# Delta rule in a four-layer network: later places for the transfers of the inverse's blocks, two buffers for the inverse, four for its input

## The chip, the cores and the metric

One core of one Trainium2 chip runs the whole program once. The metric is the time of that execution in microseconds (us), as the median of several runs. A profiled execution is shown beside it; all rows below are from that one execution.

## The reference

The network has four layers on 272 tokens (16 learned ones and 256 given), then a second network of two blocks. Layers 0 and 3 mix tokens with a gated delta rule, and only these two call what is changed. For each of 8 heads, in chunks of 64 tokens:

```python
a_strict = where(strict, (k*beta) @ k.T * decay, 0)     # lower triangle
m = a_strict + eye
u = triangular_solve(m, v * beta)
w = triangular_solve(m, k * beta * exp(gc))
# then over the chunks, with a state S (128 x 128) of each head:
v_new = u - w @ S
o = (q * exp(g)) @ S + (q @ k.T * decay) @ v_new
S = S * exp(g_last) + (k * exp(g_last - g)).T @ v_new
```

q, k, v come from one projection of the normalised input, a causal convolution over four tokens, SiLU and a norm; o is normalised, gated by z and projected back to the residual h.

## The kernel before

A stage of the program is one layer: `dn0`, `mlp0`, `da1`, `mlp1`, `lru2`, `mlp2`, `dn3`, then the second network (`blk2`). In a delta stage (`_dn`) the input projection is cut into 16 weight chunks of 1 MB, in the order of `DN_ORDER`: k0 k1 v0 q0 k2 v1 q1 k3 z0 v2 q2 v3 q3 z1 z2 z3. The number is a pair of heads; there are four pairs. A chunk is loaded by SP's queue into `wraw` (three buffers), split by ScalarE and VectorE into a high and a low part (`whi`, `wlo`, three buffers each, line 418 and 421), and used in 48 matmuls into `pm` (line 392). So each stage has 16 x 48 of them, and then 4 x 48 of the output projection (`proj_out`, chunks `dno`): 960.

For each pair the chunk of 128 tokens is the unit of the solve (and the 16 learned tokens are a small one). `dn_keys` forms the strict triangle U (matmuls `ga`, VectorE writes `U`); `dn_blocks` inverts its 16 x 16 diagonal blocks; `dn_merge` joins them to the inverse `Y` by matmuls `gp` and `pp` (six steps in turn, each needs VectorE's or ScalarE's result of the one before); `dn_chain` runs the recurrence (`pvm`, `sp`, then `ksp`, `pv`, `spn`, `po` for either chunk), and `dn_tail` norms, transposes (`oT`) and gates the output for `proj_out`.

`dn_blocks` goes through DRAM to bring blocks to partitions: SP stores U to `ud` (line 940) and loads `X` from it (942); GpSimd (POOL) does 15 steps of elimination on X into `yb` (947 to 954); SP stores `yb` to `yd` (957) and loads `yc` (959), from which `dn_merge` starts. `X` and `yb` have one buffer each.

These are Python generators, one task each. `mm3` calls `tick()` after every eighth matmul, and a tick lets every task run to its next `yield`; `yield n` sleeps n ticks. `finish(task)` ticks, with no matmul between, until a task is done. This makes the order in which the program is written. It is not the order in which the engines get it: the framework that builds the program fills each engine's queue itself, taking what it reckons to be ready, and the earliest written first. On the chip each queue is then worked in that fixed order.

Waits in the written order: `dn_keys` of pair p waits, before U, until the inverse of pair p-2 is merged (there are two `fx` sets, pair p uses set p % 2; one Y for all), and `dn_merge` of pair p waits until pair p-1 has used Y (`solved`).

Of the kernel before, what the change touches and what calls it, by code (L numbers as in the profile page):

```python
# [9 lines left out]
F32 = mybir.dt.float32  # L10
# [290 lines left out]
class Prog:  # L301
# [56 lines left out]
    def act(self, out, a, func, **k):  # L358
        i = self.S.activation(out=out, in_=a, func=func, **k).ins  # L359
        if func in (AF.Exp, AF.Ln):  # L360
            if self.table is not None:
                self.order(i, self.table)
        elif func in (AF.Silu, AF.Sqrt):
            self.other = i
        return i
# [168 lines left out]
    def _dn(self, s, layer, last, e):  # L534
        nc, A, d1 = self.nc, self.A, self.d1
        t0 = NM if last else 0
        w0 = self.chunk(A[f"dnA{s}"][0])
        self.dnc = d1.tile([P, _DNC.n], F32, name="dnc")
        nc.sync.dma_start(out=self.dnc, in_=A["dnc"])
        u, R = self.normed(self.h, f"nmix{layer}", T)  # L540
        y = [d1.tile([P, 4, T], F32R, name=n)[:, :, t0:T] for n in ("yh", "yl")]
        ys = [[a[:, 2 * i:2 * i + 2, :] for a in y] for i in range(2)]
        self.d2 = d2 = e(self.tc.tile_pool(name="d2", bufs=2))
        gates, ready = self.dn_gates(s, u, R)
        self.dn_fixed()
        conv = f"dnconv{s}"
        zs = d1.tile([P, 8, T], F32, name="zs")
        chains, outs, self.ms = [], [], {}
        self.solved = 0
        self.inv, keys, f = [None] * 4, [[] for _ in range(4)], {}  # L550

        def project(nm, p, w):
            ci = "kvq".index(nm)
            f[nm, p] = cv = d2.tile([P, 2, T], F32, tag=nm + "T", name=nm + "T", bufs=4 if nm == "k" else 2)
            for m in range(2):
                ps = self.pm.tile([P, 512], F32, tag="pm", name="pm")[:, 0:T]
                self.mm3(ps, w, 8, 256, m, u)
                raw = d2.tile([P, 3 + T], F32, tag="raw", name="raw")
                self.V.memset(raw[:, 0:3], 0.0)
                self.tt(raw[:, 3:], ps, R, ALU.mult)  # L560
                j = (8, 16, 0)[ci] + 2 * p + m
                self.act(cv[:, m, :], raw[:, 3:3 + T], AF.Copy, scale=self.pc(conv, 72 + j))
                for t in range(3):
                    self.stt(cv[:, m, :], raw[:, t:t + T], self.pc(conv, 24 * t + j), cv[:, m, :], ALU.mult, ALU.add)
            self.act(cv, cv, AF.Silu)
            if nm == "k":
                self.spawn(self.dn_keys(p, cv, gates, ready, keys[p]))

        tails = []
        def load(o):  # L570
            nm, p = o[0], int(o[1])
            return self.chunk(A[f"dnA{s}"][12 + p if nm == "z" else 3 * p + "kvq".index(nm)])

        order = DN_ORDER.split()
        ws = [w0]
        for i, o in enumerate(order):
            nm, p = o[0], int(o[1])
            if i + 1 < len(order):
                ws.append(load(order[i + 1]))
            w = ws[i]  # L580
            if nm != "z":
                project(nm, p, w)
                if nm == "q":
                    on = (d1.tile([P, 2, 2, P], F32, name=f"on{p}"), None if last else d1.tile([48, P], F32, name=f"om{p}"))
                    outs.append(on)
                    chains.append(self.spawn(self.dn_chain(p, f["k", p], f["v", p], f["q", p], gates, keys[p], on, last)))
                continue
            for m in range(2):
                ps = self.pm.tile([P, 512], F32, tag="pm", name="pm")[:, 0:T - t0]
                self.mm3(ps, w, 8, 256, m, (u[0][:, :, t0:T], u[1][:, :, t0:T]))  # L590
                z = d2.tile([P, 3 + T], F32, tag="raw", name="z")[:, t0:T]
                self.tt(z, ps, R[:, t0:T], ALU.mult)
                self.act(zs[:, 2 * p + m, t0:T], z, AF.Silu)
            if p > 1:
                ys.append([d2.tile([P, 2, T], F32R, tag="kT", name=n, bufs=4)[:, :, t0:T] for n in ("yh", "yl")])
            tails.append(self.spawn(self.dn_tail(s, p, chains[p], outs[p], zs, ys[p], t0)))
        ys = [[[a[:, j, :] for b in ys[g:g + 2] for a in (b[i],) for j in range(2)] for i in range(2)] for g in (0, 2)]
        self.proj_out(f"dno{s}", ys, T - t0, [[t] for t in tails], self.add_h(t0))
# [24 lines left out]
    def dn_fixed(self):  # L623

        d1, V = self.d1, self.V
        self.fx = []
        for i in range(2):
            t = dict(U=d1.tile([P, 5, P], F32, name=f"U{i}"), At=d1.tile([48, 48], F32, name=f"Atm{i}"),
                     vm=d1.tile([48, P], F32, name=f"vm{i}"), km=d1.tile([48, 2, P], F32, name=f"km{i}"),
                     Y=d1.tile([P, 4, P], F32, name="Y") if i == 0 else self.fx[0]["Y"])  # L630
            V.memset(t["U"][:, 4, :], 0.0)
            for n in ("At", "vm", "km"):
                V.memset(t[n], 0.0)
            self.fx.append(t)

    def dn_gates(self, s, u, R):
# [115 lines left out]
    def dn_ssq(self, x, out):  # L752

        sp = self.pst("ssq2")
        self.V.memset(sp[:, 4:5], 0.0)
        sq = self.d2.tile([P, 2, T], F32, tag="sq2", name="sq2", bufs=1)
        self.act(sq, x, AF.Square)
        for h, c in self.M4:
            i = 2 * h + c
            self.colsum(sp[:, i:i + 1], sq[:, h, self.CK[1 + c]])  # L760
        for h in range(2):
            self.mm(sp[self.RH[h], 4:5], sq[:, h, 0:16], self.ones[:, 0:1])
        self.V.tensor_scalar_add(out=out, in0=sp[:, 0:5], scalar1=EPS)

    def dn_keys(self, p, kT, gates, ready, keys):

        d2, mm, tt, stt, act, V = self.d2, self.mm, self.tt, self.stt, self.act, self.V
        RH, ck = self.RH, self.CK
        while not ready.done:
            yield  # L770
        rows, bet, gc, ng = gates
        fx = self.fx[p % 2]
        mneg = self.dc("mneg")
        E = d2.tile([P, 2, T], F32, tag="E", name="E")
        Dx = d2.tile([P, 4, P], F32, tag="Dx", name="Dx")
# [20 lines left out]
        V.reciprocal(out=sv, in_=kk)  # L796
        tt(sv, sv, bet[:, p, :], ALU.mult)
        yield
        while p > 1 and self.inv[p - 2] is None:
            yield  # L800
        U = fx["U"]
        ga = self.pst("ga").rearrange("p (a b) -> p a b", a=4)
        gm = self.pst("gm")
# [7 lines left out]
        for r in RH:  # L811
            stt(U[r, 4, r], gm[r, 0:16], sv[r, 4:5], Dm[r], ALU.mult, ALU.mult)
        box = []
        yield from self.dn_blocks(U, box)
        while p and self.solved < p:
            yield
        self.inv[p] = yield from self.dn_merge(U, box[0], fx["Y"])

    def dn_chain(self, p, kT, vT, qT, gates, keys, outs, last):
# [1 line left out]
        M4, RH, ck = self.M4, self.RH, self.CK  # L821
        rows, bet, gc, ng = gates
        on, om = outs
        fx = self.fx[p % 2]
        while len(keys) < 5 or self.solved < p - 1:
            yield
        E, Dx, Dm, sk, sv = keys
# [41 lines left out]
        for h in range(2):  # L869
            r = RH[h]  # L870
            act(ke[:, h, :], kp[:, h, :], AF.Copy, scale=Dx[:, 2 * h, P - 1:P])
            act(km[r, h, :], kp[r, 2, :], AF.Copy, scale=Dm[r, 15:16])
            act(vm[r], kp[r, 3, :], AF.Copy, scale=sk[r, 4:5])
        while self.inv[p] is None:
            yield
        Y, Ym = self.inv[p]
# [55 lines left out]
        stt(ms, ms, 1.0 / P, qf, ALU.mult, ALU.add)  # L932
        self.ms[p] = ms

    def dn_blocks(self, U, box):

        d2, dd, V, G = self.d2, self.dd, self.V, self.G
        q = self.nc.sync
        ud = dd.tile([5, 129, P], F32, tag="ud", name="ud")
        q.dma_start(out=ud[:, 0:P, :].rearrange("m p c -> p m c"), in_=U)  # L940
        X = d2.tile([40, 16, 16], F32, tag="X", name="X", bufs=1)
        q.dma_start(out=X, in_=bass.AP(ud.tensor, ud.offset, [[2064, 40], [P, 16], [1, 16]]))
        yb = d2.tile([40, 16, 2, 16], F32, tag="yb", name="yb", bufs=1)
        yield 6
        t = d2.tile([40, 15, 16], F32, tag="t16", name="t16", bufs=1)
        Y = yb[:, :, 0, :]
        G.memset(Y, 0.0)
        G.memset(yb.rearrange("p a t b -> p (a t b)")[:, 0:512:33], 1.0)
        for k in range(15, 0, -1):
            n = 16 - k  # L950
            o = t[:, 0:k, 0:n]
            G.tensor_tensor(out=o, in0=X[:, 0:k, k:k + 1].broadcast_to([40, k, n]), in1=Y[:, k:k + 1, k:16].broadcast_to([40, k, n]), op=ALU.mult)  # L952
            G.tensor_tensor(out=Y[:, 0:k, k:16], in0=Y[:, 0:k, k:16], in1=o, op=ALU.subtract)  # L953
        G.tensor_copy(out=yb[:, :, 1, :], in_=Y.rearrange("p a b -> p b a"))
        yield 10
        yd = dd.tile([40, 16, 2, 16], F32, tag="yd", name="yd")
        q.dma_start(out=yd, in_=yb)
        yc = d2.tile([P, 5, 2, 16], F32, tag="yc", name="yc")
        q.dma_start(out=yc.rearrange("p m t c -> p m (t c)"), in_=bass.AP(yd.tensor, yd.offset, [[32, P], [4096, 5], [1, 32]]))
        box.append(yc)  # L960
        yield 8

    def dn_merge(self, U, yc, Y):

# [947 lines left out]
```

## Time and profile before

| | us |
|---|---|
| median of 3 runs | 2575.45 (2573.39 to 2577.97) |
| profiled execution: its own time | 2578.68 |
| profiled execution: span of the rows | 2576.5 |
| TensorE (PE) busy in the span | 2520.1 (98%) |
| stage dn0, first gate matmul to end of pair 3's `oT` | 7.1 to 210.3 |
| stage dn3, the same | 1034.6 to 1226.9 |

Rows give times in us from the start of the span, and durations in us unless ns is written. PE is TensorE's matmuls, PEld its weight loads, DVE VectorE, ACT ScalarE, POOL GpSimd, SP the engine whose queue issues the transfers; a q behind an engine means its queue. A row such as `72.21 0.65 PE L392 MATMUL gp<-yw,U ... x32 [3.48 <-...]` is 32 matmuls of line 392 that write `gp` from `yw` and `U`, began at 72.21, took 0.65, after 3.48 in which the engine stood idle; what released it is named behind the arrow, by the profile's inference.

### The profile page before, as it was taken

How to read it: one execution, taken by the hardware profiler on the slowest of the kernel's cores; microseconds unless marked ns; L12 is line 12 of the kernel's file. 1: busy time of each engine (PE TensorE's matmuls, PEld its weight loads, DVE VectorE, ACT ScalarE, POOL GpSimd, SP SyncE). 2: the span in 40 equal slices, each digit the busy share in tenths (PEclk: the TensorE clock that was granted, in tenths of full speed). 3: DMA queues.
4: the chain of work that ended last, by engine and by line, in shares of the span. 5: the costliest groups of instructions: out<-in, count | busy, mean ns of one | idle time of the engine just before them, and what ended most of it. 6: DMA issues, size and time to landing. Idle time of an engine off the chain costs nothing.

```text
span 2576.5 us, 54055 instructions
## 1 busy us (share of the span) xinstructions
PE 2520.1 (98%) x21942; PEld 2449.5 (95%) x21942; DVE 2044.8 (79%) x4613; ACT 1469.6 (57%) x2544; POOL 119.8 (5%) x280
## 2 busy tenths in 40 slices
PE   8899999999999999989999999999999999999998
PEld 8789999999999999979999999999878999999998
DVE  8678967779779976857996887886767978987765
ACT  8776445664457644868654544644655445545544
POOL 1420001000000000331000000000000000000000
PEclk9899999999999999989999999999999999999999
DMA  4326755347545764323875665564314865974553
GB/s 173 114 95 233 281 180 178 132 180 262 196 147 182 262 229 168 116 99 128 291 295 181 234 245 176 197 213 168 128 60 163 325 246 195 327 257 148 180 187 108
DMA packets 89577, 494.56 MB, mean 192 GB/s; under 512 B 18448, under 2 KB 28336, under 8 KB 33264
## 3 DMA queue, kind: packets, MB, share of 16 engines
q1 hardware_dynamic: 89328, 491.10, 54.2%
q8 instruction: 173, 2.83, 0.4%
q14 instruction: 76, 0.62, 0.1%
HBM read 485.10 MB, written 5.96 MB: 191 GB/s over the span
## 4 chain that ended last, share of the span: by engine, by line
PE 88%; DVE 3%; POOL 3%; ACT 2%; DMA 2%; issue 1%; SPq 0%; DVEq 0%; ACTq 0%; POOLq 0%
PE pm L392 81%; POOL t L952 1%; POOL yb L953 1%; PE o L392 1%; DVE wlo L421 1%; ACT L359 1%; DMA wraw<-dnA 1%; PE sp L392 1%; PE ssq L392 0%; PE ga L392 0%; DMA crow<-crow 0%; PE po L392 0%; PE oT L402 0%; DMA X<-ud 0%; ACT whi L418 0%
## 5 line engine op out<-in xcount | busy, mean ns | idle before, releaser
L418 ACT CAST whi<-wraw 128x1024 fp32r<-128x1024 f32 (+1 forms) x767 | 768.8, 1033 | 556.3 <-PE pm L392 319.1
L392 PE MATMUL pm<-ul,whi 128*128 128x258 f32 (+2 forms) x3768 | 1084.2, 288 | 1.5 <-DVE ul L409 0.8
L392 PE MATMUL pm<-uh,whi 128*128 128x258 f32 (+2 forms) x3768 | 1080.2, 287 | 2.9 <-ACT uh L359 2.3
L392 PE MATMUL pm<-uh,wlo 128*128 128x258 f32 (+2 forms) x3768 | 1081.2, 288 | 0.2 <-DVE wlo L421 0.2
L421 DVE TENSOR_TENSOR wlo<-wraw,whi 128x512 fp32r<-128x512 f32 x1511 | 984.2, 690 | 95.5 <-ACT whi L418 92.4
L392 PEld LDWEIGHTS pm<-uh,whi 128*128 128x128 f32 x3768 | 714.5, 190 | 8.3 <-ACT uh L359 2.7
L392 PEld LDWEIGHTS pm<-ul,whi 128*128 128x128 f32 x3768 | 714.3, 190 | 7.5 <-issue 2.8
L392 PEld LDWEIGHTS pm<-uh,wlo 128*128 128x128 f32 x3768 | 714.7, 190 | 6.6 <-issue 4.3
L392 PE MATMUL pm<-hh,wlo 128*128 128x256 f32 (+1 forms) x1904 | 541.5, 284 | 0.0
L392 PE MATMUL pm<-hh,whi 128*128 128x256 f32 (+1 forms) x1904 | 541.4, 284 | 0.0
L392 PE MATMUL pm<-hl,whi 128*128 128x256 f32 (+1 forms) x1904 | 540.4, 284 | 0.0
L392 PEld LDWEIGHTS pm<-hl,whi 128*128 128x128 f32 x1904 | 361.0, 190 | 0.0
L392 PEld LDWEIGHTS pm<-hh,wlo 128*128 128x128 f32 x1904 | 359.0, 189 | 0.0
L392 PEld LDWEIGHTS pm<-hh,whi 128*128 128x128 f32 x1904 | 358.2, 188 | 0.0
L1395 DVE SCALAR_TENSOR_TENSOR wmod<-wmod,crow 128x1024 f32<-128x1024 f32 x144 | 174.1, 1214 | 0.1
L356 DVE TENSOR_TENSOR h<-h,pm 128x272 f32<-128x272 f32 (+1 forms) x192 | 81.8, 428 | 83.4 <-PE pm L392 82.8
L408 ACT CAST hh<-t 128x256 fp32r<-128x256 f32 x110 | 44.5, 405 | 146.0 <-DVE t L353 145.7
L359 ACT ACT_TABLE_LOAD x88 | 112.9, 1283 | 10.0 <-DMA crow<-crow 7.4
L359 ACT ACTIVATE s<-r 128x272 f32<-128x272 f32 (+1 forms) x128 | 53.7, 425 | 71.5 <-DVE r L353 70.3
L359 ACT ACTIVATE t<-t,b 128x256 f32<-128x256 f32 x110 | 55.5, 507 | 64.8 <-DVE t L356 64.7
L356 DVE TENSOR_TENSOR t<-pm,rstd 128x256 f32<-128x256 f32 x220 | 90.6, 413 | 0.0
L353 DVE SCALAR_TENSOR_TENSOR h<-pm,gate,h 128x256 f32<-128x256 f32 x96 | 46.1, 480 | 49.8 <-PE pm L392 49.7
(453 smaller groups left out, 2699.8 us busy)
## 6 DMA issues: line engine op xcount, KB each, us to landing
wraw<-mlp SPq DMA_DIRECT2D x128, 1024.0 KB, 4.9
wmod<-wmod SPq DMA_DIRECT2D x72, 1024.0 KB, 6.3
wraw<-f1i SPq DMA_DIRECT2D x66, 1024.0 KB, 4.8
wraw<-f2i SPq DMA_DIRECT2D x44, 1024.0 KB, 4.9
wraw<-dnA SPq DMA_DIRECT2D x32, 1024.0 KB, 4.9
wraw<-f1o SPq DMA_DIRECT2D x24, 1024.0 KB, 4.8
wraw<-f2o SPq DMA_DIRECT2D x16, 1024.0 KB, 4.8
wraw<-daA SPq DMA_DIRECT2D x12, 1024.0 KB, 4.9
```

The source lines that it names most:

```text
L353: self.V.scalar_tensor_tensor(out=out, in0=a, scalar=s, in1=b, op0=op0, op1=op1)
L356: self.V.tensor_tensor(out=out, in0=a, in1=b, op=op)
L359: i = self.S.activation(out=out, in_=a, func=func, **k).ins
L392: self.PE.matmul(out=out, lhsT=lhsT, rhs=rhs, start=start, stop=stop)
L408: self.S.copy(out=hi, in_=x)
L418: self.S.copy(out=hi[:, k], in_=raw[:, k])
L421: self.V.tensor_sub(out=lo[:, k], in0=raw[:, k], in1=hi[:, k].bitcast(F32))
L952: G.tensor_tensor(out=o, in0=X[:, 0:k, k:k + 1].broadcast_to([40, k, n]), in1=Y[:, k:k + 1, k:16].broadcast_to([40, k, n]), op=ALU.mult)
L953: G.tensor_tensor(out=Y[:, 0:k, k:16], in0=Y[:, 0:k, k:16], in1=o, op=ALU.subtract)
L1395: i = self.V.scalar_tensor_tensor(out=junk, in0=w[:, k, :], scalar=1.0, in1=c[:, r, :], op0=ALU.mult, op1=ALU.mult, accum_out=m[:, j:j + 1])
```

## The change

`dn_blocks` gets the pair's number and sleeps differently. Before: store ud, load X, 6 ticks, POOL, 10 ticks, store yd, load yc, 8 ticks. After: store ud, 4 ticks, wait until the pair before has left POOL's part (`blocked`), load X, 3 ticks, POOL, 16 ticks, store yd, 3 ticks, load yc, 4 ticks. There are four U (one for each pair) and two Y. `dn_keys` no longer waits for the inverse of pair p-2, but for the reads of `dn_chain` of pair p-2 (`read`). `dn_merge` of pair p waits for the merge of pair p-1 and for pair p-2's use of Y. `sq2` shares its buffer with `yf`, which gives back part of the space.

```diff
-        self.solved = 0
+        self.solved = self.read = self.blocked = 0
...
-        for i in range(2):
-            t = dict(U=d1.tile([P, 5, P], F32, name=f"U{i}"), At=d1.tile([48, 48], F32, name=f"Atm{i}"),
-                     vm=d1.tile([48, P], F32, name=f"vm{i}"), km=d1.tile([48, 2, P], F32, name=f"km{i}"),
-                     Y=d1.tile([P, 4, P], F32, name="Y") if i == 0 else self.fx[0]["Y"])
+        for i in range(4):
+            t = dict(self.fx[i - 2]) if i > 1 else dict(
+                At=d1.tile([48, 48], F32, name=f"Atm{i}"), vm=d1.tile([48, P], F32, name=f"vm{i}"),
+                km=d1.tile([48, 2, P], F32, name=f"km{i}"), Y=d1.tile([P, 4, P], F32, name=f"Y{i}"))
+            for n in ("At", "vm", "km") if i < 2 else ():
+                V.memset(t[n], 0.0)
+            t["U"] = d1.tile([P, 5, P], F32, name=f"U{i}")
             V.memset(t["U"][:, 4, :], 0.0)
-            for n in ("At", "vm", "km"):
-                V.memset(t[n], 0.0)
...
-        sq = self.d2.tile([P, 2, T], F32, tag="sq2", name="sq2", bufs=1)
+        sq = self.d2.tile([P, 2, T], F32, tag="yf", name="sq2", bufs=1)
...
-        while not ready.done:
+        while not ready.done or self.read < p - 1:
             yield
...
-        fx = self.fx[p % 2]
+        fx = self.fx[p]
...
-        while p > 1 and self.inv[p - 2] is None:
-            yield
         U = fx["U"]
...
-        yield from self.dn_blocks(U, box)
-        while p and self.solved < p:
+        yield from self.dn_blocks(p, U, box)
+        while p and (self.solved < p - 1 or self.inv[p - 1] is None):
             yield
...
+        self.read = p + 1
         while self.inv[p] is None:
             yield
...
         q.dma_start(out=ud[:, 0:P, :].rearrange("m p c -> p m c"), in_=U)
+        yield 4
+        while self.blocked < p:
+            yield
         X = d2.tile([40, 16, 16], F32, tag="X", name="X", bufs=1)
         q.dma_start(out=X, in_=bass.AP(ud.tensor, ud.offset, [[2064, 40], [P, 16], [1, 16]]))
...
-        yield 6
+        yield 3
...
-        yield 10
+        yield 16
+        self.blocked = p + 1
         yd = dd.tile([40, 16, 2, 16], F32, tag="yd", name="yd")
         q.dma_start(out=yd, in_=yb)
+        yield 3
...
-        yield 8
+        yield 4
```

## Rows read from the trace of the kernel before

**Rows 1.** The page, part 1: busy time, share of the span, instructions.

```profile
PE 2520.1 (98%) x21942; PEld 2449.5 (95%) x21942; DVE 2044.8 (79%) x4613; ACT 1469.6 (57%) x2544; POOL 119.8 (5%) x280
```

**Rows 2.** Windows: length, busy PE, PEld, DVE, ACT, POOL; clock, DMA share, GB/s.

```profile
60.00:100.00 40.00, 32.17 (x436) 28.18 (x435) 25.77 (x77) 26.19 (x51) 16.75 (x47) 0.83 0.38 124
...
160.00:212.00 52.00, 52.00 (x563) 48.13 (x562) 35.01 (x84) 38.04 (x95) 0.00 (x0) 1.00 0.34 111
...
1090.00:1130.00 40.00, 27.97 (x371) 25.20 (x370) 20.34 (x58) 19.91 (x37) 16.48 (x33) 0.74 0.27 93
```

**Rows 3.** Timeline of PE: the long waits inside the two stages.

```profile
72.21 0.65 PE L392 MATMUL gp<-yw,U 32*32 32x32 f32 x32 [3.48 <-DVE raw L559]
...
89.96 1.11 PE L392 MATMUL gp<-yt,U 64*64 64x64 f32 x8 [4.35 <-ACT yt L359]
...
125.12 0.66 PE L392 MATMUL pp<-Y,gs 64*64 64x64 f32 x5 [1.64 <-ACT gs L1027]
...
1115.11 1.11 PE L392 MATMUL gp<-yt,U 64*64 64x64 f32 x8 [11.83 <-ACT yt L359]
```

**Rows 4.** Timeline of ACT before the second and the fourth of these.

```profile
88.28 1.04 ACT L418 CAST whi<-wraw 128x1024 fp32r<-128x1024 f32 x1 [4.72 <-DMA wraw<-dnA]
...
1113.43 1.04 ACT L418 CAST whi<-wraw 128x1024 fp32r<-128x1024 f32 x1 [12.38 <-DMA wraw<-dnA]
```

**Rows 5.** Timeline of SP's queue: transfers in the order of issue.

```profile
44.71 0.34 SPq L415 DMA_DIRECT2D wraw<-dnA  x1
45.15 0.35 SPq L942 DMA_DIRECT2D X<-ud  x1
...
81.55 0.29 SPq L957 DMA_DIRECT2D yd<-yb  x1
81.95 0.34 SPq L415 DMA_DIRECT2D wraw<-dnA  x1
...
1108.23 1.41 SPq L415 DMA_DIRECT2D wraw<-dnA  x3
```

**Rows 6.** Waits of SP's queue, 0 to 240 and 1030 to 1240: total, times, longest.

```profile
SPq L957 <- POOL yb L954: 37.4, 4, 13.9
...
SPq L957 <- POOL yb L954: 50.1, 4, 20.6
```

**Rows 7.** Windows of POOL's run of pair 1, in dn0 and in dn3.

```profile
67.30:81.60 14.30, 10.82 (x186) 10.11 (x185) 9.26 (x31) 9.78 (x16) 11.71 (x33) 0.76 0.20 72
...
1086.30:1106.00 19.70, 16.77 (x276) 15.25 (x274) 17.98 (x51) 14.23 (x23) 17.29 (x31) 0.97 0.13 50
```

**Rows 8.** Windows of the tile pm alone in dn0: PE, PEld, DVE, ACT.

```profile
12.50:72.20 59.70, 45.79 (x331) 42.57 (x331) 4.94 (x12) 0.00 (x0) 0.99 0.42 139
72.30:171.90 99.60, 55.80 (x325) 46.64 (x325) 6.54 (x16) 0.00 (x0) 0.91 0.34 110
172.00:198.20 26.20, 16.66 (x106) 14.05 (x107) 1.74 (x4) 0.00 (x0) 1.00 0.24 81
```

**Rows 9.** The chain that ended last, end of dn0: start, us, what.

```profile
198.28 10.92 PE pm L392 x87
209.20 1.06 PE oT L402 x6
```

**Rows 10.** Windows of the stretches at half clock: one, and the four's sum.

```profile
125.30:132.10 6.80, 6.80 (x37) 5.73 (x37) 3.63 (x11) 4.41 (x10) 0.00 (x0) 0.50 0.26 81
...
sum 40.80, PE 27.03 PEld 24.16 DVE 11.11 ACT 20.06 POOL 6.96; mean PE 6.76 PEld 6.04 DVE 2.78 ACT 5.01 POOL 1.74
```

**Rows 11.** Groups of ACT and DVE, 171.9 to 212: count, busy us, mean ns.

```profile
L359 ACT ACTIVATE on<-on,ms 128x128 f32<-128x128 f32 x12 | 3.9, 392 | 0.5 <-DVE ms L606 0.4
L359 ACT ACT_TABLE_LOAD x3 | 3.8, 1283 | 0.1
...
L353 DVE SCALAR_TENSOR_TENSOR yf<-oT,par,zs 128x272 f32<-128x272 f32 x6 | 3.0, 500 | 3.5 <-PE oT L402 3.3
...
L409 DVE TENSOR_TENSOR yl<-yf,yh 128x544 fp32r<-128x544 f32 x3 | 2.2, 721 | 0.3 <-ACT yh L408 0.3
```

More of the change, by code (lines that the diff above doesn't have):

```diff
@@ L823, in dn_chain @@
         on, om = outs
-        fx = self.fx[p % 2]
+        fx = self.fx[p]
         while len(keys) < 5 or self.solved < p - 1:
@@ L933, in dn_chain, with dn_blocks @@
         self.ms[p] = ms
-    def dn_blocks(self, U, box):
+    def dn_blocks(self, p, U, box):
         d2, dd, V, G = self.d2, self.dd, self.V, self.G
```

## The prediction

> **What bounds the kernel now.** I read the page's busy times first. PE is busy 98% of the span and POOL 5% [rows 1], so a change to POOL's transfers can only give back time in which PE stands still or runs slowly. Windows of the two delta stages show where that is: in the 40 us from 60 and in the 40 us from 1090 PE misses 7.8 and 12.0 us and the clock is granted at 0.83 and 0.74; late in the stage, from 160 to 212, PE misses nothing [rows 2]. PE's timeline gives the waits: 3.48, 4.35 and 1.64 us in dn0 and 11.83 us in dn3, 21.3 us together, all in front of a step of `dn_merge` [rows 3].
>
> The arrow behind the 4.35 and the 11.83 points at ScalarE's `yt`. Going one step back, ScalarE itself had stood 4.72 and 12.38 us at the cast of a weight chunk that had not arrived [rows 4]; it works in order, so `yt` stood behind that cast. Another step back, SP asked for that chunk at 81.95 and 1108.23, directly after the store of yd of pair 1 (and, in dn3, the load of yc) [rows 5]. And SP's waits say why so late: the store of yd stood 13.9 us and 20.6 us for POOL, 37.4 and 50.1 us over the four pairs of a stage [rows 6]. POOL's run of pair 1 takes 14 us in dn0 and 20 us in dn3 [rows 7]. So the chain is POOL, yd at the head of SP's queue, weight load, cast, merge, PE. The 1.64 and the 3.48 us are in front of merge steps too, and I take them for yc that comes late.
>
> Behind each wait the granted clock was at half: four stretches, 40.8 us, PE busy in 27.0 [rows 10], at 0.50, the lower of the two levels (1.2 GHz). At the upper one that work needs 13.5 us less. All that could be given back is then 21.3 + 13.5 = 34.8 us, 1.4% of the span, and any other cost must be set against this.
>
> **The change part by part.** It adds no matmul and no transfer; it moves them in the written order. That is not the order of the queues: the load of a weight chunk that is written four chunks behind X was issued before X [rows 5]. So a later place does not by itself delay a transfer on SP, which is mostly free when the builder picks; the place decides among things that are ready together. On PE, where `pm` matmuls are nearly always ready, it decides a lot.
>
> I counted ticks from the yields (8 `pm` matmuls to a tick, 960 in a stage). Before, the first `gp` of pairs 0 to 3 is written at matmul 296, 408, 544 and 656; after, at 344, 496, 648 and 860. The counted rows agree for the last pair: 331 + 325 = 656 stand before its `gp`, and 331 before pair 0's, which came 35 later than written [rows 8]. Later pairs come out later because the pairs now go through POOL's part one at a time, 3 + 16 = 19 ticks each.
>
> (1) *The early stalls.* Pair 0's `gp` moves from 331 to at least 344, 13 matmuls of 126 ns (10.92/87 [rows 9]), 1.6 us; U of pair 2 with its matmuls comes before it, some 1.2 us (8 matmuls like `oT`'s six in 1.06). Of the 3.48 + 4.35 that leaves some 5; in dn3 18 matmuls and the same U take 3.5 from 11.83. The 1.64, with its stretch of half clock (6.8 busy, so 3.4 [rows 10]), goes: POOL's run of pair 2 no longer waits for a merge, since U has a buffer of its own, and is done long before merge 2. Of the other half clock (10.1) I take 3. Sum: 2.8 + 3.5 + 1.6 + 3.4 + 3 = 14.3; I take 15. The bounds are 0 (SP's order as before) and 34.8 (every stall gone).
>
> Whether more goes hangs on one thing: yd of pair 1 and the next weight load stand side by side in SP's queue [rows 5]. If the later place of yd lets the load pass, both long waits vanish; if the builder reckons POOL's run shorter than the 14 to 20 us [rows 7], yd stays in front. Nothing in the trace of before tells which.
>
> (2) *The end of the stage.* Pair 3's merge is now written at matmul 860, the rest of it behind 888, and from there `finish(tail 3)` ticks 16 times with no matmul between. The last 72 of `proj_out` need that pair. Before, all this stood among 106 `pm` matmuls and PE missed nothing [rows 2, 8]. That PE takes the earlier written first is seen at `oT` of pair 3: 87 matmuls of 10.92 us stand between the last `po` and it [rows 9], in the place that the ticks give (848). So the cover is gone.
> Price of one stage: the 26.2 us from pair 3's `gp` to its last `po` hold 106 x 0.126 = 13.3 of `pm`; of the 12.9 left 2.1 are two other pairs' `oT` and 1.4 eight `kp` by the same price, so 9.4 is PE's part of merge and chain. Bounds of merge and chain without cover: 9.4, as if nothing stood between steps, and 26.2, as now. I take 15.4: 12 steps in turn with 0.5 between (one DVE operation of 500 ns, or an ACT one of 392 ns and a hand-over [rows 11]); this is nearer the lower end, as the steps themselves are short. The tail: table load 1.28, five `on` 1.96, `oT` 1.06, two `yf` 1.0, split 2 x 0.72, three tiny ones 0.6: 7.3 [rows 9, 11]. Together 22.7. Against it stand PE's work that is no longer done earlier (9.4 + 1.06 = 10.5) and 28 matmuls that still lie beside it (3.5): 8.7 us. Such a gappy stretch would fall to the lower clock, as after every wait of 1.6 us and more [rows 3, 10]: half of the 10.5 again, 5. One stage loses 13.7, two 27. Bounds: 9.4 + 7.3 - 14.0 = 2.7 and 26.2 + 7.3 - 14.0 + 10.5 = 30 for a stage, 5 and 60 for two.
>
> (3) *Nothing:* the memsets of two more U and a Y fewer wait lie at the start of the stage under the first loads; `sq2` in the buffer of `yf` makes pair 2's `sq2` wait for pair 0's split, written 8 ticks earlier; the wait for `read` is met when it is asked (chain 0 has read at tick 31, pair 2's keys come at 34). If a cover is gone here, the first to be late is a `pg` or an `ssq` by under 1 us.
>
> Sum: 27 - 15 = +12 us. Against the profiled execution's own 2578.68 that is 2590.7; it lies 3.2 above the median, so 2587.
>
> The Trainium skill, "DMA: Bandwidth & Descriptors", section "Rules for kernel authors", advises to issue a transfer early, compute, and wait late, and so speaks against this change. By that alone part 1 is worth nothing, and the time would be 2575 + 27 = 2602, the third rival below; SP's 13.9 us at yd speak against it, as a transfer asked for before its data exist stops the ones behind it.
>
> **The rivals.**
> *Load passes yd* (faster): yd of pair 1 falls behind the weight load in SP's queue, ScalarE never stands at the cast, and all 34.8 us come back. For it: load and yd are neighbours [rows 5], and the yd of after is written at tick 57 and that load at 51, where it was 34 and 51. Against: merge and load both still depend on POOL's speed. With a loss at the end between 17 and 27: -18 to -8, about 2562. It decides for faster from a loss of under 30 us.
> *No bare end* (faster): the builder finds holes on PE between matmuls 760 and 860 and puts pair 3's steps there. Then only part 1 counts: -15, 2560. Against it stands `oT` of pair 3, which found no hole in 87 matmuls [rows 9].
> *Asked later, nothing else* (slower): SP's order stays and yd stops the same loads at the same times, since POOL's runs set them: +20 to +27, 2599.
> *No change to be measured:* one stage's order flips and the other's doesn't, gain 25 against loss 27, or both parts are small: within 5 us, 2575.
>
> **How the numbers follow.** What a measurement of this kernel can tell from no change is about 0.2%, 5 us. Forecast 2587: 0.34. Load passes yd: 0.30. No bare end: 0.08. Asked later, nothing else: 0.09. No change: 0.19. So faster 0.38, same 0.19, slower 0.43. The cases reach from 2557 (all stalls gone, end at 17) to 2602; I give 2556 to 2602. The forecast's own range is 2580 to 2597: gains from 10 to 20, loss from 22 to 32.
>
> **What would show it.** In the profile after: PE's wait in front of `gp` from `yt` in dn3, 3 to 9 us if part 1 is right, none if the load passes yd, 12 if nothing changes; SP's wait of L957 for POOL below 37.4 and 50.1, or not; POOL's run of pair 2 directly behind pair 1's. For part 2: from pair 3's `gp` in either stage some 20 to 30 us in which PE has gaps between `gp`, `pp`, `pv` and `po` with no `pm` among them, at a granted clock of 0.5, and the last 72 `pm` of `proj_out` behind them. The prediction is wrong if pair 3's merge stands among `pm` matmuls again, or if its bare steps take under 17 us.

## The result, and the profile after

The changed kernel takes 2611.66 us (2611.15 to 2612.32), the kernel before 2576.64 on the same chip (2573.39 to 2577.97): ratio 1.0138, 95% interval 1.012 to 1.0156. That is slower, as forecast; but 35 us slower, where the forecast said 12, and outside the range given. Its profiled execution took 2612.32 us, its span is 2610.1.

The page after, part 1, beside [rows 1]. The work is the same, so PE's share falls:

```profile
PE 2527.8 (97%) x21942; PEld 2454.3 (94%) x21942; DVE 2046.9 (78%) x4617; ACT 1471.4 (56%) x2546; POOL 123.1 (5%) x280
```

To see where the 35 us are, cut both traces at the same work: from the first `ssq` matmul of a delta stage to the first `ssq` matmul of what follows. Windows of before (length, PE, PEld, DVE, ACT, POOL; clock, DMA share, GB/s):

```profile
17.30:229.70 212.40, 201.32 (x2253) 183.04 (x2251) 158.13 (x444) 163.46 (x343) 52.19 (x130) 0.95 0.38 129
1036.90:1247.60 210.70, 197.29 (x2264) 181.24 (x2262) 157.15 (x446) 160.28 (x329) 56.46 (x130) 0.95 0.38 129
```

and of after, first the same two stages, then each stage cut where pair 3's first `gp` comes, up to the next `pm` behind its chain:

```profile
16.90:244.70 227.80, 202.69 (x2246) 183.34 (x2244) 158.19 (x443) 163.22 (x343) 56.77 (x130) 0.92 0.36 122
1052.50:1282.90 230.40, 205.36 (x2250) 187.17 (x2249) 157.49 (x448) 159.76 (x328) 55.03 (x130) 0.89 0.35 118
...
16.90:200.10 183.20, 168.41 (x1907) 152.71 (x1905) 137.30 (x394) 138.88 (x285) 56.77 (x130) 0.94 0.36 121
200.10:229.60 29.50, 19.18 (x232) 15.59 (x231) 8.82 (x23) 12.19 (x36) 0.00 (x0) 0.76 0.22 72
1052.50:1238.00 185.50, 170.03 (x1913) 155.50 (x1913) 135.64 (x396) 136.96 (x274) 55.03 (x130) 0.93 0.34 112
1238.00:1267.50 29.50, 19.93 (x234) 16.48 (x232) 9.97 (x25) 11.35 (x32) 0.00 (x0) 0.70 0.24 92
```

The stages are 15.4 and 19.7 us longer, 35.1 together, and the whole spans differ by 33.6 (2610.1 less 2576.5): all of the difference is here. PE's idle time (length less busy) goes from 11.1 to 25.1 us in dn0 and from 13.4 to 25.0 in dn3, and the clock falls from 0.95 to 0.92 and 0.89. Of this, 10.3 and 9.6 us lie in the 29.5 us behind pair 3's `gp`, where before PE missed nothing in dn0 [rows 2]; what lies ahead of them grew too, to 14.8 and 15.5.

That end, PE's timeline in dn0 (rows of pair 3's steps, the `pm` between 200.5 and 204.3 left out):

```profile
200.13 0.45 PE L392 MATMUL gp<-yw,U 32*32 32x32 f32 x32
...
205.51 0.44 PE L392 MATMUL gp<-yw,U 32*32 32x32 f32 x16 [0.52 <-DVE yw L356]
206.31 0.50 PE L392 MATMUL pp<-yw,gs 32*32 32x32 f32 x3 [0.36 <-ACT gs L1015]
...
207.69 0.68 PE L392 MATMUL gp<-yt,U 64*64 64x64 f32 x8 [0.66 <-ACT yt L359]
...
214.11 1.22 PE L392 MATMUL pv<-rr,Y 128*128 128x128 f32 x4 [0.44 <-DVE rr L353]
...
226.55 0.28 PE L402 MATMUL oT<-ident,om 16*128 16x16 f32 x1 [4.48 <-ACT om L359]
...
229.55 1.28 PE L392 MATMUL pm<-yh,whi 128*128 128x272 f32 x4 [1.27 <-ACT yh L408]
```

From 204.3 to 229.55 there is no `pm` at all: step after step of merge, chain and tail waits for VectorE or ScalarE, and the tail's `oT` longest.

The beginning of the stage, SP's waits in dn0 and in dn3, beside [rows 6] (total, times, longest):

```profile
SPq L961 <- POOL yb L957: 46.5, 4, 17.3
...
SPq L961 <- POOL yb L957: 43.9, 4, 17.0
```

SP's queue at the chunk that came late, the tenth, and ScalarE at the cast of the ninth (72.79) and of the tenth, beside [rows 5] and [rows 4]:

```profile
83.47 0.29 SPq L961 DMA_DIRECT2D yd<-yb  x1
83.86 0.34 SPq L415 DMA_DIRECT2D wraw<-dnA  x1
...
72.79 1.98 ACT L418 CAST whi<-wraw 128x1024 fp32r<-128x1024 f32 x2
88.98 1.99 ACT L418 CAST whi<-wraw 128x1024 fp32r<-128x1024 f32 x2 [14.21 <-DMA wraw<-dnA]
90.99 1.28 ACT L359 ACT_TABLE_LOAD   x1
92.28 0.66 ACT L359 ACTIVATE vT<-vT 128x544 f32<-128x544 f32 x1
92.84 0.92 ACT L359 ACTIVATE qT<-raw,par 128x272 f32<-128x272 f32 x2
```

VectorE at the low part of the ninth, and ScalarE at the cast of the tenth in dn3:

```profile
77.44 1.88 DVE L421 TENSOR_TENSOR wlo<-wraw,whi 128x512 fp32r<-128x512 f32 x3
93.38 2.56 DVE L353 SCALAR_TENSOR_TENSOR qT<-raw,par,qT 128x272 f32<-128x272 f32 x6 [14.06 <-ACT qT L359]
95.87 0.76 DVE L421 TENSOR_TENSOR wlo<-wraw,whi 128x512 fp32r<-128x512 f32 x1
...
1127.00 1.04 ACT L418 CAST whi<-wraw 128x1024 fp32r<-128x1024 f32 x1 [14.58 <-DMA wraw<-dnA]
```

and what PE then waits for in the two stages, beside [rows 3]:

```profile
96.68 0.59 PE L392 MATMUL pm<-uh,wlo 128*128 128x272 f32 x1 [13.95 <-DVE wlo L421]
...
1133.74 0.58 PE L392 MATMUL pm<-uh,wlo 128*128 128x256 f32 x1 [13.43 <-DVE wlo L421]
```

Pair 1's yd still stands directly in front of the weight load. The merge waits of 3.48, 4.35 and 11.83 us are gone from the merge. In their place each stage has one wait, of 13.95 and 13.43 us. It ends with the piece of `wlo` at 95.87, which is not of the late chunk: a chunk's low part is written in four pieces, and this is the 36th of the stage's 16 chunks, so the last of the ninth, whose cast was done by 74.8. The piece stands in VectorE's queue behind six operations on `qT`; these wait for ScalarE, and ScalarE stands at the cast of the late tenth chunk.

### The profile page after: what moved, and what is told of

Read it like the earlier page. It is cut to its first block, busy times and chain, and to the rows that moved or that the text cites. A ratio compares the mean times of both kernels' runs of the same rounds, so it can differ in the third digit from the quotient of the medians.

```text
span 2610.1 us, 54079 instructions
## 1 busy us (share of the span) xinstructions
PE 2527.8 (97%) x21942; PEld 2454.3 (94%) x21942; DVE 2046.9 (78%) x4617; ACT 1471.4 (56%) x2546; POOL 123.1 (5%) x280
## 4 chain that ended last, share of the span: by engine, by line
PE 89%; DVE 3%; ACT 3%; POOL 2%; DMA 1%; issue 1%; SPq 0%; DVEq 0%; ACTq 0%; POOLq 0%
PE pm L392 81%; POOL yb L956 1%; POOL t L955 1%; PE o L392 1%; PE sp L392 1%; PE po L392 1%; DVE wlo L421 1%; PE pp L392 1%; ACT L359 1%; PE ssq L392 1%; PE ga L392 0%; PE oT L402 0%; ACT whi L418 0%; PE gp L392 0%; PE pv L392 0%
## 5 line engine op out<-in xcount | busy, mean ns | idle before, releaser
L392 PE MATMUL pm<-yh,whi 128*128 128x272 f32 (+1 forms) x288 | 83.6, 297 | 4.4 <-ACT yh L408 4.3
```

The costliest lines, as they stand in the source:

```text
L392: self.PE.matmul(out=out, lhsT=lhsT, rhs=rhs, start=start, stop=stop)
```

## The experiments

Each is compared with the kernel before on its own chip.

**One half of the change at a time (e1 to e4).** *Buffers alone*: four U, two Y, `read` and the new condition of the merge, with the old sleeps:

```diff
-        yield 4
-        while self.blocked < p:
-            yield
...
-        yield 3
+        yield 6
...
-        yield 16
+        yield 10
...
-        yield 3
...
-        yield 4
+        yield 8
```

> Only the buffers and their waits of the change (four U, two Y, read, the merge's new condition); sleeps 6, 10, 8 and no wait for blocked, as before. Pair 3's first gp is written at matmul 608 of 960, no bare ticks at the end. Theory 'places' (the loss is the later places of the block transfers, which leave the last pair without pm beside it; the early wait is set by POOL and SP): 2570 to 2584, no gaps at the end, the early waits of 9 to 14 us per stage still there. Theory 'buffers' (U of pair 2 and its work come earlier in VectorE's queue and make the early wait longer): 2590 to 2605.

*Sleeps alone*: those lines of the new `dn_blocks`, `blocked` too, on the kernel before.

> Only the sleeps 4, 3, 16, 3, 4 and the wait for blocked, in the kernel before with its two U and one Y. Pair 3's first gp is written at 860, 16 bare ticks. 'Places': 2602 to 2614, the end without cover in both stages, about 10 us of PE's idle time in each. 'Buffers': 2570 to 2582.

*Without `blocked`*: the changed kernel, of which only this is taken out:

```diff
-        while self.blocked < p:
-            yield
```

> The changed kernel without the wait for blocked; sleeps and buffers as changed. Pair 3's first gp is written at 656, as before, and no tick is bare. 'Places': 2574 to 2590, the end covered. 'Buffers': 2600 to 2612.

*A sleep of 8*: the changed kernel with `yield 8` for `yield 16`.

> The changed kernel with 8 ticks in place of 16 behind POOL's part; a pair then holds the next by 11 ticks, and pair 3's first gp is written at 592. 'Places': 2568 to 2586, the end covered, early waits still 9 to 14 us per stage. 'Buffers': 2600 to 2612.

| | us, median | ratio | 95% |
|---|---|---|---|
| buffers alone | 2586.38 | 1.0050 | 1.003 to 1.007 |
| sleeps alone | 2621.95 | 1.0190 | 1.0173 to 1.0206 |
| without `blocked` | 2577.99 | 1.0018 | 1.0007 to 1.0029 |
| a sleep of 8 | 2584.83 | 1.0047 | 1.0031 to 1.0063 |

Two lines carry the loss: without the wait for the pair before, 31 of the 35 us are gone (0.0120 of 2576). They are the end of the stage, because the early wait stands there as in the changed kernel; PE's timeline without `blocked`:

```profile
97.52 0.59 PE L392 MATMUL pm<-uh,wlo 128*128 128x272 f32 x1 [14.01 <-DVE wlo L421]
...
1117.74 0.58 PE L392 MATMUL pm<-uh,wlo 128*128 128x256 f32 x1 [13.04 <-DVE wlo L421]
```

and its stages by the same cut as above (windows):

```profile
17.70:229.50 211.80, 196.95 (x2253) 179.33 (x2251) 157.34 (x444) 164.29 (x344) 54.56 (x130) 0.95 0.38 130
1036.90:1249.50 212.60, 196.48 (x2263) 180.53 (x2262) 157.68 (x449) 160.62 (x329) 55.33 (x130) 0.94 0.39 128
```

They measure 211.8 and 212.6 us, so the bare ends cost 227.8 - 211.8 = 16.0 and 230.4 - 212.6 = 17.8. The sleeps alone, above the range expected of them, show the same 4.48 in front of dn0's last `oT` and 15.19 us of early wait. The buffers alone were not nothing either: half a per cent is lost, a little more than expected. Their profile has merge waits of 8.3 and 6.8 us; what the loss comes from was not taken apart. A sleep of 8 covers the end too (no wait in front of `oT` is left) and still loses 12 us, with merge waits of 10.9 and 6.5.

**A store that lets one load pass, or another queue (e5 to e8).** If the place of yd on SP's queue made the early wait, moving it should take the wait away. e5 on the changed kernel, and e6 on the one without `blocked`, put the store behind the last weight load written:

```diff
-        q.dma_start(out=yd, in_=yb)
+        self.order(q.dma_start(out=yd, in_=yb).ins, self.load)
```

(e6 also lets pair 1 wait until nine loads are written.) Both put one load more, 10 for 9, in front of pair 1's store; e5 also puts pairs 2 and 3 behind 14 and 16 loads, 12 and 15 in the changed kernel.

> The changed kernel, and in SP's queue the store of yd is held behind the weight load written last before it (for pair 1 that of chunk 9). Theory 'queue' (the early wait of 14 us in dn0 and 13 in dn3 is yd of pair 1, which waits for POOL in front of that load): both waits shrink to under 3 us and their half clock goes, 2611 falls to 2575 to 2590; the end without cover stays. Rival 'POOL' (POOL's run of 15 to 20 us is itself late for the merge, whoever stands in front): a wait of 8 us and more stays in front of gp or pp, 2600 to 2612.

> The changed kernel without the wait for blocked (the end is covered), with yd held behind the load as in the run before it, pair 1's also written behind the load of chunk 9. 'Queue': early waits and end both gone, 2535 to 2560, faster than before. 'POOL': 2570 to 2585.

e7 on the kernel before, and e8 on the changed one without `blocked`, issue all four transfers of `dn_blocks` from POOL's queue:

```diff
-        q = self.nc.sync
+        q = self.nc.gpsimd
```

> The kernel before, with the four block transfers (ud, X, yd, yc) issued by POOL's queue instead of SP's. 'Queue': SP's loads are never held, the waits of 4.4 us in dn0 and 11.8 us in dn3 go, 2545 to 2562. 'POOL': the transfers and POOL's run are as long or longer, 2570 to 2585.

> The changed kernel without the wait for blocked, and the four block transfers on POOL's queue. 'Queue': early waits and end both gone, 2535 to 2560. 'POOL': 2570 to 2590.

| | us, median | ratio | 95% |
|---|---|---|---|
| one load ahead, changed kernel | 2611.61 | 1.0142 | 1.0119 to 1.0166 |
| one load ahead, without `blocked` | 2576.84 | 1.0005 | 0.9991 to 1.0019 |
| POOL's queue, kernel before | 2581.56 | 1.0032 | 1.0019 to 1.0044 |
| POOL's queue, without `blocked` | 2577.03 | 1.0009 | 0.9997 to 1.0022 |

None gained what the queue theory expected. The traces say why. With one load ahead, that chunk is on time and the next one is the late one. SP's queue and ScalarE of e5:

```profile
68.02 0.47 SPq L416 DMA_DIRECT2D wraw<-dnA  x1
87.49 0.29 SPq L963 DMA_DIRECT2D yd<-yb  x1
...
90.30 0.46 SPq L416 DMA_DIRECT2D wraw<-dnA  x1
...
96.06 1.99 ACT L420 CAST whi<-wraw 128x1024 fp32r<-128x1024 f32 x2 [15.43 <-DMA wraw<-dnA]
```

With the transfers on POOL's queue SP waits for POOL nowhere, and then it is the merge that stands: VectorE and PE of e7,

```profile
75.81 0.26 DVE L356 TENSOR_TENSOR Ym<-yc,dnc 48x48 f32<-48x48 f32 x1 [7.81 <-DMA yc<-yd]
...
76.61 0.65 PE L392 MATMUL gp<-yw,U 32*32 32x32 f32 x32 [7.51 <-DVE raw L559]
```

So the plain form of the queue theory fell, and two were left: POOL's run itself is too long, or one load is too short a distance.

**A shorter run of POOL (e9 to e12).** Some of the elimination is left out, so the inverse is not the whole one:

```diff
-        for k in range(15, 0, -1):
+        for k in range(15, 0, -2):
```

on the kernel before, on the changed one, and on the one without `blocked`; e12 steps by -4 on the kernel before.

> The kernel before with every second of POOL's 15 elimination steps left out (8 stay; the inverse of the 16x16 blocks is then not the whole one). POOL theory (the early waits come from the length of POOL's run, wherever the transfers behind it are queued): POOL's run falls from 14 to 20 us to some 8 to 11, the early waits of a stage (9.5 and 11.8 us) fall to under 5, with the half clock behind them the time is 2545 to 2562. Queue theory (a transfer's place, not POOL's length): the waits stay over 8 us, 2570 to 2580.

> The changed kernel with the same half of POOL's steps left out. POOL theory: the early waits of 14 and 13 us fall to under 7, the bare end of 29 us stays in both stages, so 2580 to 2598: it is still 25 to 40 us behind the kernel before with the same half left out. Queue theory: the waits stay over 11 us and the time at 2605 to 2615.

> The changed kernel without the wait for the pair before, with the same half of POOL's steps left out. POOL theory: early waits under 7 us instead of 14 and 13, no bare end: 2550 to 2565. Queue theory: waits as before, 2572 to 2582.

> The kernel before with only 4 of POOL's 15 elimination steps (k = 15, 11, 7, 3). POOL theory: POOL's run under 6 us, no early wait over 2 us, 2535 to 2552, about 5 to 15 us below the kernel with 8 steps. Queue theory: as with 8 steps, within 5 us of the kernel before.

| | us, median | ratio | 95% |
|---|---|---|---|
| half, kernel before | 2540.90 | 0.9873 | 0.9853 to 0.9892 |
| half, changed kernel | 2592.59 | 1.0065 | 1.0048 to 1.0082 |
| half, without `blocked` | 2555.63 | 0.9925 | 0.9898 to 0.9951 |
| quarter, kernel before | 2540.89 | 0.9868 | 0.9851 to 0.9885 |

With half of POOL's steps the kernel before gives back 35 us (2575.68 - 2540.9), the whole of the 34.8 that the prediction counted in waits and half clock. Windows of e9 on the two stretches of [rows 2]:

```profile
60.00:100.00 40.00, 39.29 (x534) 34.03 (x523) 34.81 (x103) 34.64 (x75) 15.94 (x38) 1.00 0.38 123
1090.00:1130.00 40.00, 39.58 (x492) 35.42 (x492) 30.12 (x92) 34.16 (x78) 10.40 (x28) 1.00 0.36 110
```

e9's whole stages, by the same cut as above:

```profile
17.10:213.40 196.30, 193.95 (x2252) 176.59 (x2250) 156.54 (x444) 163.26 (x343) 30.43 (x74) 1.00 0.41 140
1020.80:1214.10 193.30, 192.32 (x2264) 177.25 (x2262) 155.89 (x447) 160.23 (x329) 28.20 (x74) 1.00 0.43 141
```

Against the stages of before 21.2 us of PE's idle time and 12.3 us of its busy time are gone, where the prediction counted 21.3 and 13.5. A quarter gives no more: nothing is left to give. And even with a short run the changed kernel's places cost: 52 us more than the same half on before, 37 of it gone without `blocked`, 15 left, with early waits of 3.0 and 3.7 us in e11. But these kernels leave work out, and their order on SP's queue differs too.

**All the work, on VectorE (e13 to e15).** The 33 instructions of a pair on VectorE instead of POOL: on the kernel before, there for pair 1 alone, and on the one without `blocked`.

```diff
-        d2, dd, V, G = self.d2, self.dd, self.V, self.G
+        d2, dd, V, G = self.d2, self.dd, self.V, self.V
```

> The kernel before with all of POOL's 33 instructions of a pair on VectorE instead, the whole work done. VectorE does small operations in 0.16 to 0.22 us where POOL takes 0.2 to 0.9. Theory of POOL's length: the run of a pair falls from 14 to 20 us to 5 to 9, the early waits to under 4 us in a stage, 2542 to 2562. Rival (VectorE works in order, so 5 to 9 us of elimination, and its wait for X, stand in front of the split of weight chunks; a new wait takes the old one's place): waits of 5 to 10 us in a stage at pm from wlo, 2565 to 2590.

> The kernel before with the 33 instructions of pair 1 alone on VectorE, the others on POOL. Theory of POOL's length: pair 1's run ends some 10 us earlier, the wait behind the weight chunk (4.4 and 11.8 us) goes, pair 0's wait (3.5) may stay: 2545 to 2565. Rival (VectorE in order, a new wait): 2568 to 2585.

> The changed kernel without its wait for the pair before, with all of POOL's instructions on VectorE. Theory of POOL's length: early waits under 4 us and no bare end, 2542 to 2565, not better than the kernel before with the same move, as the later places have nothing left to give. Rival (the later places help once the run is short): 5 us or more below that kernel. Rival (VectorE in order): 2565 to 2590.

| | us, median | ratio | 95% |
|---|---|---|---|
| all on VectorE, before | 2562.38 | 0.9956 | 0.9941 to 0.9971 |
| pair 1 on VectorE, before | 2568.80 | 0.9987 | 0.9977 to 0.9997 |
| all on VectorE, without `blocked` | 2559.16 | 0.9943 | 0.9928 to 0.9957 |

The first and the third came out at or in their range, though not for the reason given; pair 1 alone gave little, with waits of 5 us left in either stage. VectorE does one of these in 0.15 to 0.22 us, yet works on other things between: pair 0's run lasts from 50.5 to 67.9 and pair 1's from 70.6 to 87.9, 17 us each, no shorter than POOL's 14 in the same stage [rows 7]. PE's idle time still fell, to 5.2 and 7.7 us in the two stages. What differs is the queue: in dn0 pair 1's store stands behind 11 loads (in dn3 behind 12), where it stood behind 9 before. SP's timeline of e13:

```profile
68.95 0.36 SPq L415 DMA_DIRECT2D wraw<-dnA  x1
...
79.27 0.33 SPq L415 DMA_DIRECT2D wraw<-dnA  x1
87.92 0.30 SPq L957 DMA_DIRECT2D yd<-yb  x1
```

Two loads stand between pair 0's store (67.90) and pair 1's here; in the trace of before there is one, at 65.90.

**Two loads ahead, POOL unchanged (e16 to e18).** e16 on the kernel before and e17 on the changed one without `blocked` put pair 1's store behind 11 loads; e18 is e17 with pair 0's behind 9 as well, 8 before.

```diff
+        while p == 1 and self.loads < 10:
+            yield
...
-        q.dma_start(out=yd, in_=yb)
+        self.order(q.dma_start(out=yd, in_=yb).ins, self.load)
```

(The lines are e17's. e16 orders pair 1's store alone; e18 has `while p < 2 and self.loads < 8 + 2 * p`.)

> The kernel before, pair 1's store of yd ordered behind 11 loads of weight chunks in SP's queue (9 before, 10 in the runs with one load ahead), POOL's run unchanged. Theory of the distance (one load was not enough, the second one covers POOL's run): no early wait over 4 us, 2552 to 2566. Theory of POOL (the merge comes late whatever stands ahead, and a wait of 8 to 14 us appears one load further): 2570 to 2585.

> The changed kernel without its wait for the pair before, pair 1's store of yd behind 11 loads (9 and 10 in the runs before it). Theory of the distance: no early wait over 4 us instead of 14 and 11, 2552 to 2566. Theory of POOL: a wait of 8 to 14 us one load further, 2570 to 2585.

> As the kernel with 11 loads ahead of pair 1's store on the changed kernel without its wait, and pair 0's store behind 9 loads (8 before): nearly the places of the kernel with the steps on VectorE. Theory of the distance: 2550 to 2564, within 5 us of the one with pair 1 alone. Theory of POOL: 2570 to 2585.

| | us, median | ratio | 95% |
|---|---|---|---|
| two loads ahead, before | 2595.52 | 1.0089 | 1.0061 to 1.0118 |
| two loads ahead, without `blocked` | 2556.10 | 0.9937 | 0.9919 to 0.9956 |
| the same, pair 0's too | 2556.27 | 0.9938 | 0.9922 to 0.9955 |

e17 and e18 do all the work with POOL's run as it was, and are the fastest such kernels here, 19 us below before by the medians. SP's queue of e18 in order of time, and among it two casts: at 75.51 that of the tenth chunk, at which ScalarE stood 4.72 us in [rows 4] and now does not stand, and at 81.40 that of the eleventh:

```profile
64.81 0.30 SPq L964 DMA_DIRECT2D yd<-yb  x1
...
69.78 0.47 SPq L416 DMA_DIRECT2D wraw<-dnA  x1
...
75.51 2.00 ACT L420 CAST whi<-wraw 128x1024 fp32r<-128x1024 f32 x2
...
76.52 0.34 SPq L416 DMA_DIRECT2D wraw<-dnA  x1
...
81.40 2.00 ACT L420 CAST whi<-wraw 128x1024 fp32r<-128x1024 f32 x2 [1.10 <-DMA wraw<-dnA]
...
84.49 0.30 SPq L964 DMA_DIRECT2D yd<-yb  x1
```

Its stages by the same cut as above (windows):

```profile
17.70:214.80 197.10, 195.41 (x2253) 177.24 (x2251) 159.00 (x444) 167.00 (x346) 51.95 (x130) 1.00 0.42 139
1022.20:1226.50 204.30, 196.61 (x2263) 180.18 (x2262) 158.31 (x449) 162.67 (x330) 53.09 (x130) 0.98 0.40 133
```

POOL still ends pair 1 at 84.5, but two chunks were asked for meanwhile, and in dn0 PE misses 1.7 us. In e17 the wait has not gone quite: 4.87 and 8.57 us of it stand one load further, more than the 4 expected. Its time came as the distance theory said, its waits between the two theories; they are those of its profiled execution, the slowest of its eight (2563.62, median 2556.10).

e16 missed, and by the other half of the story. Its edit waits in the written order, and on the kernel before, where pairs share U and Y, this delays pair 3 as well: its store comes at 170.34, where it came at 149.86 before, and its end is bare again. PE and SP of e16:

```profile
170.34 0.30 SPq L961 DMA_DIRECT2D yd<-yb  x1
...
228.48 0.28 PE L403 MATMUL oT<-ident,om 16*128 16x16 f32 x1 [4.48 <-ACT om L360]
```

## Why the prediction was wrong

**What bounds the kernel** was right. Behind the waits was the length of POOL's run with yd at the head of SP's queue: with half the run the counted 34.8 us came back as 35, and with the run whole, two loads ahead of yd gave back 19. Of the 23 us by which the forecast was short, 20 are step (1) and 4 step (2), each rounded.

**Step (1), the early stalls, failed.** Its term was a gain of 15 us, worked out by taking 2.8, 3.5 and 1.6 us off the waits in front of the merge and 6.4 off the half clock behind them, as if a later `gp` waited less and nothing else changed. The waits in front of the merge did go, the 3.48 and the 1.64 for good. In the place of the 4.35 and the 11.83 came 13.95 and 13.43 in front of `pm`, and not for the late chunk's data: behind its cast stood what PE needed next, as `yt` did before. The wait up to that cast did not shrink. In dn0 the cast came at 88.98 (88.28 before), and PE stood from 82.7, where before it stood only from 85.6 (89.96 less 4.35), since pair 0's merge and its 3.48 us of waiting lay ahead. In dn3 it was the other way: PE stood 6.7 us before the cast, 10.2 before the change. Together these are 12.9 us, 12.8 before. What grew stands behind the cast. Before, PE's next work needed `yt`, which ScalarE wrote soon behind it, and PE went on 1.7 us after the cast began [rows 3, 4]. Now it needs the last piece of the ninth chunk's `wlo`. In VectorE's queue six operations on `qT` stand in front of that, and these wait for ScalarE, which does the cast, a table load, `vT` and its own part of `qT` first. This takes 7.7 us in dn0 and 6.7 in dn3, 14.4 for 3.4 before: 11 us more, against the 5 that went. This is read from the timelines; no run changed that order by itself.

So PE's idle time ahead of the end went from 11.1 to 14.8 us in dn0 and from 13.4 to 15.5 in dn3. Without the bare end the whole change measures 1.0018, a loss of about 5 us (in the profiles 1.3: 6.5 us more idle time, 5.2 less busy time). The step should have read -5, not +15, below its lower bound of 0, which took an unchanged order on SP to cost nothing. The text had named the point on which it hangs, that yd stays in front if the builder reckons POOL's run too short; SP's order did stay. It then credited a gain that needs no such pass. Its sign for a load that passed, no wait in front of `gp` in dn3, came without it: the wait had moved to `pm`.

**Step (2), the end of the stage, was right in mechanism and small in size.** Pair 3's merge came behind the `pm` of its place, steps with gaps of 0.4 to 0.7, the last `pm` of `proj_out` behind them. The term was 27 us; it measured 16.0 + 17.8 = 33.8 in the profiles, 31 by the ratios, inside 5 to 60. Against e3 the two stages have 19.2 us more idle time, where the step had 17.4 (twice 8.7), and PE is busy 14.6 us longer with the same work at a lower granted clock, where it had 10 (twice 5). So the term that was mis-sized is the clock's: 10.5 us of work take 10.5 more at the lower level, the step took half of that, 5, and 7.3 a stage was measured. The tail was sized well: from the end of the last `po` (222.1) to the next `pm` it took 7.5 us, against 7.3. From pair 3's `gp` to that `po` it was 21.9 us, the slower clock included, where the term had 15.4 without it.

The Trainium skill's advice in "DMA: Bandwidth & Descriptors", section "Rules for kernel authors", to issue early and wait late, gave 2602: nearer than the forecast, as part (1) was indeed worth nothing here. But it is half of the matter here: e17 and e18 put the store of yd behind two more loads and are faster by 0.6%, and what they issue earlier by this is the weight chunk.

**Step (3)**, nothing for the buffers, held for what it names: in the trace after no `pg` or `ssq` waits in either stage. But the freer order that they allow cost 1.005 with the old sleeps, which no step had.

**The rivals.** *Asked later, nothing else* (2599) was what happened, with a larger bare end and a small loss in front: by the ratios 2575 + 31 + 5 is 2611, beside 2611.66. *Load passes yd* was right in its mechanism, yet one load was not enough: e5 to e8 show nothing, e17 and e18 are 21 us below e3 by the ratios, where this rival gives back 34.8. *No bare end* and *No change to be measured* fell.

Two small slips moved nothing: the forecast's own range begins at 2577 (2575 + 22 - 20) and not 2580, and eight matmuls at the price of `oT` are 1.4 us and not 1.2.

What stays open: in e17 waits of 4.87 and 8.57 us are left and in e18 none over 1.9, though their medians agree. One difference is seen on SP: in e18 the next load follows pair 1's store at once (84.90 and 1093.72), in e17 the load of yc stands between, and it is asked for at 91.95 and 1108.12. Whether this is the cause, and why the medians agree all the same, was not tried. The edits on yd's place also move the written places of merges, and that part was not tried by itself.

## What to carry to other kernels

A late place in a written order has a price at the end of the stage: count what is left to lie beside the last item's chain before moving anything later, since two lines cost 31 us here by letting it run out. A store that waits for a slow producer holds every load behind it in its queue; look at how many loads the producer's run lasts (two here), because letting only one pass moved the wait to the next load and gained nothing (e5, e6). And when a queue stands at late data, all behind it is late, whatever it needs itself: moving one instruction that waited is no gain unless the data come earlier or nothing else that is needed stands there. Ask what stands first behind it then, and how much work lies between (1.7 us before, 6.7 and 7.7 after).

## What was unexpected

VectorE took 0.15 to 0.22 us for each small elimination step, POOL 0.21 to 3.34 with a median of 0.33, and still a pair's run took 17 us on VectorE, as its other work stood between the steps; yet the kernel was 0.44% faster. With PE never idle for long (e9), the granted clock of both stages was 1.00; with the early waits alone it was 0.95 (the kernel before), and with the bare ends as well 0.92 and 0.89.
